# Three rewrites of a hybrid GDN / differential-attention layer and a later place for the projection's stores

## The chip, the cores and the metric

The kernel runs on one core of a Trainium2 chip, as one program with one launch. The metric is the device time of a run in microseconds (us), the median of several runs. A core has five instruction queues that run beside each other, each in its own order: PE (TensorE, matrix products and transposes), ACT (ScalarE), DVE (VectorE), POOL (GpSimd) and SP, which here issues every DMA transfer. Matrix results land in PSUM, in eight banks of 128 x 512 float32; everything else stands in SBUF or in DRAM.

## The reference

One decoder layer with 2048 tokens, model width 1024 and two groups of four heads that read the same normalised input, all in float32:

```python
hn = rms_norm(x, w_norm)
proj = einsum("bsd,de->bse", hn, w_in)          # q_a k_a v_a z_a b_a a_a q_b k_b v_b z_b
# A: gated DeltaNet, 4 heads, chunks of 64
qkv = silu(causal_depthwise_conv(q_a|k_a|v_a, conv_w)); q_a, k_a = l2_norm(..), l2_norm(..)
a_mat = tril(k_beta k^T * decay, -1) + I
u, w = solve_triangular(a_mat, [v_beta, k_beta * exp(g)])
state = state * exp(g_last) + k_dec^T (u - w state);  o_a = q_dec state + tril(q k^T * decay) v_new
o_a = rms_norm(o_a, gdn_norm_w) * silu(z_a)
# B: differential attention, 4 heads, two 64-wide maps each, causal
q_b, k_b = rope(rms_norm(q_b)), rope(rms_norm(k_b))
p = softmax(q1 k1^T / 8) - lam * softmax(q2 k2^T / 8);  o_b = p v_b
o_b = rms_norm(o_b, subln_w) * (1 - lam_init) * silu(z_b)
out = x + concat(o_a, o_b) w_out
```

## The kernel before

**How products are made.** A float32 operand is used in one of two ways. As plain float32 a product is issued as one matrix instruction that the chip runs as two passes (the profile shows both). Or it is split into a high part that TensorE reads in its reduced float32 form (`fp32r`) and the rest, and the product is the sum of three single passes: high x high, high x rest, rest x high. The projection, the scores, the output product and the chunk products of part A are three-product sums; the attention's second product (probabilities x values, "AV"), the triangular inverse and the state scan are plain float32.

**Stages.** (1) `x_scale` and `x_split` normalise and transpose the input; `in_proj` runs three passes over column groups of `w_in` and halves of the tokens. One job is one PSUM bank `psi` (three of them) of 24 or 48 matrix instructions. Three generators `epilogue` take the jobs in turn; each has one buffer `raw` and one `acc`, evicts the bank on ACT, works on it, and stores it to DRAM (`za_s`, `gdx`, `qk`, `v`, `zb_s`). An epilogue begins its next job only when its store has landed. (2) Part A runs beside the projection: `gdn_a` makes chunk products, `gdn_fs` inverts the 32 x 32 diagonal blocks on DVE, `gdn_comp` loads them back in another layout, `gdn_inv` joins 32 to 64 and 64 to 128 for each of 32 units (16 chunks x 2 head pairs), `gdn_scan` carries the state, `gdn_out` norms, gates and stores. (3) When both are done, attention runs over 32 units of 256 queries (four heads x blocks b = 0..3, then four heads x b = 4..7): `att_scores`, `att_exp`, `att_combine` (p1 and p2 are scaled and summed), `att_tr` (transposes and evicts p as `th`), `att_mm` (AV), `att_norm`. The output product `out_mm` fills PE's gaps and makes the end.

**What sets the order.** All stages are Python generators, and `Flow` (lines 34 to 223) is a planner that runs them: every `yield engine, wait, condition` is a piece for one engine; the planner holds a modelled clock for each engine and takes the piece that could start first (rounded to 100 ns, then by priority). The instructions are recorded in that order, and each engine runs its own queue strictly in that order, SP too. So a modelled wait shifts where an instruction stands, and nothing else.

**Names.** `psi`, `psb`, `pss`, `psg`, `tp` are PSUM tiles; `hh`/`hl` the split input, `wh`/`wl` the split weights, `wr` the raw ones; `vv` a value tile; `Ti`, `Tn`, `z` (z1, z2), `comp`, `lr` belong to the inverse. All matrix instructions go through one helper (L140, transposes L152), all ACT, DVE and POOL instructions through another (L81), all transfers through L161, so the profile's groups are told apart by tile names.

Of the kernel before, what the change touches and what calls it, by code (L numbers as in the profile page):

```python
# [12 lines left out]
ALU = mybir.AluOpType  # L13
# [213 lines left out]
def hybrid_kernel(ctx: ExitStack, tc: tile.TileContext, x, w_norm, w_in, conv_w, a_log, dt_bias,  # L227
# [23 lines left out]
    v_s = [dram.tile([S, 2 * P], F32, name=f"v_{j}") for j in range(2)]  # L251
# [12 lines left out]
    NOW = -5000  # L264

# [109 lines left out]
    NW, NX5, NXB, NTI, NLR = 264, 3, 2, 4, 4  # L375
# [254 lines left out]
    def epilogue(par, of):  # L630
        t_f = 0.0
        for n in range(par, NJ, of):
# [9 lines left out]
            if kind == GA:  # L642
# [12 lines left out]
                yield "SP", None, None  # L655
# [3 lines left out]
            elif kind == GD_:  # L659
# [19 lines left out]
                yield "SP", None, None  # L679
# [3 lines left out]
            elif kind == GQ:  # L683
# [44 lines left out]
                yield "SP", None, None  # L728
# [4 lines left out]
            elif kind == GV:  # L733
                vv = raw([P, 2, 256])
                act.activation(vv, ps.rearrange("p (t c) -> p t c", t=2), AF.Copy)
                fl.release("I")
                yield "SP", None, None
                ts_ = slice((t0 + what[0]) * P, (t0 + what[0] + 2) * P)
                t_f = dma(out=v_s[arg][ts_, :].rearrange("(t p) d -> p t d", p=P), in_=vv)
                n_v[arg] += 1  # L740
            else:
                ac = acc([P, TB])
                act.activation(ac, ps, AF.Silu)
                fl.release("I")
                yield "POOL", None, None
                pool.tensor_tensor(out=ac, in0=ac, in1=sub.to_broadcast([P, TB]), op=ALU.mult)
                yield "SP", None, None
                t_f = dma(out=zb_s[arg * 2 + what][:, ts_], in_=ac)
                n_zb[arg * 2 + what] += 1
# [193 lines left out]
    def gdn_fs():  # L943

        for sg_ in range(2):
# [20 lines left out]
            dma(out=d_s[sg_][:, 0], in_=T.rearrange("p j i -> p (j i)"))  # L966
            t_fs[sg_] = dma(out=d_s[sg_][:, 1], in_=X.rearrange("p j i -> p (j i)"))
            n_fs[0] += 1

    n_comp, t_comp = [0], [0.0]  # L970

    def gdn_comp():
        for ib in range(4):
            yield "SP", (lambda: t_fs[ib // 2]), lambda: n_fs[0] > ib // 2 and n_T[0] >= 8 * ib
            for h in range(H):
                if h % 2 == 0:
                    comp[h // 2] = ga.tile([P, 2, 4, 2, 32], F32, name=f"comp{h // 2}")
                for a in range(4):
                    r0 = h * 32 + a * 8 + ib % 2 * 4
                    t_comp[0] = dma(out=comp[h // 2][a * 32:(a + 1) * 32, h % 2].rearrange("p c t i -> p (c t) i"),  # L980
                                    in_=d_s[ib // 2][r0:r0 + 4].rearrange("c t (j i) -> j (c t) i", i=32), run=32)
                yield "SP", NOW, None
            n_comp[0] += 1
# [52 lines left out]
    def gdn_inv():  # L1036

        yield "POOL", NOW, lambda: n_fs[0] > 0  # L1040
        z1 = ga.tile([P, 2, 2, 32], F32, name="z1")
        z2 = ga.tile([P, 2, 64], F32, name="z2")
        nc.gpsimd.memset(z1, 0.0)
        nc.gpsimd.memset(z2, 0.0)
        last = None
        for u in units_b + [None]:
            t_d = t_z = t_n = 0.0
            if u is not None:
                c, hp = u
                yield "POOL", (lambda: t_comp[0]), lambda: n_comp[0] > c // 4 and len(Tt) < NTI  # L1050
                dl, du = (comp[hp][:, :, c % 4, i] for i in range(2))
# [5 lines left out]
                Tn = ga.tile([64, 2, 64], F32, name="Tn", bufs=2)  # L1057
                pool.tensor_tensor(out=Tn.rearrange("p h (a i) -> p h a i", i=32),
                                   in0=dl[:64, :, None, :].to_broadcast([64, 2, 2, 32]),
                                   in1=blk[:64, None, 0:2, None].to_broadcast([64, 2, 2, 32]), op=ALU.mult)  # L1060
                t_n = fl.after("ACT")
                yield "PE", (lambda: max(LR[hp, c][1], last[3] if last else 0.0)), lambda: (hp, c) in LR, "+G"
                lr = LR[hp, c][0]
            else:
                yield "PE", (lambda: last[3]), None, "+G"
            p1_ = ps_g.tile([P, 2, 96], F32, name="psg")
            if u is not None:
                for hh in range(2):
                    mm(out=p1_[:64, hh, 64:], lhsT=lr[:, hh, 64:], rhs=dl[:, hh], start=True, stop=True)
            if last is not None:  # L1070
                _, llr, lTn, _ = last
                for hh in range(2):
                    mm(out=p1_[:64, hh, :64], lhsT=llr[:64, hh, :64], rhs=lTn[:, hh], start=True, stop=True)
                live_l[0] -= 1
                t_l[0] = max(t_l[0], fl.after("SP"))
            t_1 = fl.after("DVE")
            yield AC
            if u is not None:
                act.activation(z1[32:64, :, 0], p1_[0:32, :, 64:], AF.Copy)
            if last is not None:  # L1080
                act.activation(z2[64:128], p1_[:64, :, :64], AF.Copy)
            t_z = fl.after("PE")
            if u is not None:
                yield "DVE", (lambda: t_1), None
                dve.tensor_copy(out=z1[96:128, :, 1], in_=p1_[32:64, :, 64:])
            fl.release("G")
            t_z = max(t_z, fl.after("PE"))
            yield "PE", (lambda: t_z), None, "+G"
            p2_ = ps_g.tile([P, 2, P], F32, name="psg")
            if u is not None:  # L1090
                for hh in range(2):
                    mm(out=p2_[:32, hh, 64:96], lhsT=du[:, hh], rhs=z1[:, hh, 0], start=True, stop=True)
                for hh in range(2):
                    mm(out=p2_[:64, hh, 96:], lhsT=z1[:, hh].rearrange("p b i -> p (b i)"), rhs=du[:, hh],
                       start=True, stop=True)
            if last is not None:
                lT = Tt[last[0]]
                for hh in range(2):
                    mm(out=p2_[:64, hh, :64], lhsT=z2[:, hh], rhs=lT[:, hh, 64:128], start=True, stop=True)
            t_2 = fl.after("DVE")  # L1100
            yield "ACT", (lambda: max(t_2, t_n)), None
            if last is not None:
                act.activation(lT[0:64, :, 64:128], p2_[:64, :, :64], AF.Copy)
                t_T[last[0]] = fl.after("PE")
            if u is not None:
                act.activation(Tn[32:64, :, 0:32], p2_[0:32, :, 64:96], AF.Copy)
                t_n = fl.after("PE")
                yield "DVE", (lambda: max(t_2, t_d)), None
                dve.tensor_copy(out=T[0:32, :, 32:64], in_=p2_[0:32, :, 96:])
                dve.tensor_copy(out=T[64:96, :, 96:128], in_=p2_[32:64, :, 96:])  # L1110
                last = (hp, c), lr, Tn, max(t_n, fl.after("PE"))
# [85 lines left out]
    def gdn_out():  # L1197
        for c in range(NC):
# [7 lines left out]
            rq = ga.tile([P, H], F32, name="rq")  # L1206
            rs = ga.tile([P, H], F32, name="rs")
            mh = mhalf.to_broadcast([P, H])
            pool.tensor_scalar(out=rq, in0=ssq, scalar1=EPS, scalar2=None, op0=ALU.add)
            pool.tensor_tensor(out=rq, in0=rq, in1=mh, op=ALU.pow)  # L1210
            yield PO
            pool.tensor_scalar(out=rq, in0=rq, scalar1=P ** -0.5, scalar2=None, op0=ALU.mult)
            pool.tensor_tensor(out=rs, in0=rq, in1=rq, op=ALU.mult)
            pool.tensor_tensor(out=rs, in0=rs, in1=sso, op=ALU.mult)
# [522 lines left out]
```

## Time and profile before

| | |
|---|---|
| time, median of 3 runs | 1535.0 us (1533.8 to 1536.4) |
| the profiled execution's own time | 1530.73 us |
| its span, first to last instruction | 1529.0 us |
| mean granted TensorE clock | 0.989 |
| busy: PE / DVE / ACT / POOL | 1480.3 / 958.1 / 812.4 / 497.0 us |
| DMA | 240.44 MB, 157 GB/s |

Busy time is a union: two overlapping instructions count once. Matrix instructions overlap in the pipeline, so the duration that a row gives for one (some 0.3 to 0.4 us) is longer than what it takes from the engine; the distance from one start to the next is what it costs when they run back to back. In the timeline a row is one group of equal instructions: start, length, engine, line, what is written and read, shape, count, and in brackets the idle time before it with what ended it.

### The profile page before, as it was taken

The page shows a single profiled execution, that of the slowest core. Times are in us where ns is not written, and L with a number is a line of the kernel's source. Part 1 is how long each engine was busy: PE and PEld are TensorE (multiplying, and loading weights), DVE is VectorE, ACT ScalarE, POOL GpSimd, SP SyncE. Part 2 cuts the span into 40 slices and gives each one's busy share as a digit, 9 for nine tenths or more (in the row PEclk, how much of TensorE's full clock was granted, in tenths as well). Part 3 has the DMA queues.
Part 4 walks back from the last instruction along what each step waited for, and adds up shares of the span by engine and source line. Part 5 has one row for each costly group of instructions (what it writes and reads, how often), then busy time and mean ns, then how long its engine had stood idle before and what let it go on. Part 6 is the DMA issues. An engine that isn't in the chain of part 4 may idle for free.

```text
span 1529.0 us, 27274 instructions
## 1 busy us (share of the span) xinstructions
PE 1480.3 (97%) x9671; PEld 1269.1 (83%) x9671; DVE 958.1 (63%) x2577; ACT 812.4 (53%) x1797; POOL 497.0 (33%) x616
## 2 busy tenths in 40 slices
PE   8799998999999999999999999999999999999899
PEld 6788888888789899998899899877777777877677
DVE  6466875569766667682444552227778778587782
ACT  5354464453565445323446642138777677676762
POOL 3311234500435646545353576411111122110011
PEclk8899999999999999999999999999999999999999
DMA  8758556874854774768876357256565263624224
GB/s 204 155 165 196 166 167 115 173 173 95 176 145 121 172 187 151 178 131 229 262 156 174 117 143 176 73 189 204 187 200 163 93 200 104 214 79 139 80 92 147
DMA packets 265864, 240.44 MB, mean 157 GB/s; under 512 B 46672, under 2 KB 235776, under 8 KB 263680
## 3 DMA queue, kind: packets, MB, share of 16 engines
q1 hardware_dynamic: 265728, 238.71, 57.7%
q8 instruction: 76, 1.25, 0.3%
q14 instruction: 60, 0.49, 0.1%
HBM read 150.57 MB, written 88.08 MB: 156 GB/s over the span
## 4 chain that ended last, share of the span: by engine, by line
PE 71%; DMA 10%; DVE 8%; POOL 4%; ACT 3%; issue 2%; SPq 2%; DVEq 0%; POOLq 0%; ACTq 0%
PE psi L140 32%; PE psb L140 18%; PE psg L140 7%; PE pss L140 7%; PE psb L152 4%; DMA wr<-in_w_in_dram 3%; SPq L161 2%; PE psg L152 2%; DVE p L81 2%; DMA x<-gdx 1%; DVE acc L81 1%; DMA wr<-in_w_out_dram 1%; POOL rqx L81 1%; PE tp L152 1%; POOL t L81 1%
## 5 line engine op out<-in xcount | busy, mean ns | idle before, releaser
L140 PE MATMUL psi<-wh,hh 128*128 128x256 f32 (+1 forms) x1024 | 307.7, 301 | 11.3 <-ACT acc L81 8.2
L140 PE MATMUL psi<-wl,hh 128*128 128x256 f32 (+1 forms) x1024 | 292.6, 286 | 4.7 <-DVE wl L81 4.6
L140 PE MATMUL psi<-wh,hl 128*128 128x256 f32 (+1 forms) x1024 | 291.8, 285 | 0.0
L81 DVE TENSOR_SCALAR_CACHE_REDUCE p<-pss 128x512 f32<-128x512 f32 (+3 forms) x320 | 179.3, 605 | 75.9 <-DMA kk<-qk 42.0
L140 PEld LDWEIGHTS psi<-wh,hh 128*128 128x128 f32 x1024 | 198.1, 193 | 13.0 <-ACT acc L81 8.6
L140 PE MATMUL psi<-hh,wh 128*128 128x512 f32 x512 | 206.0, 402 | 0.0
L140 PEld LDWEIGHTS psi<-wl,hh 128*128 128x128 f32 x1024 | 198.2, 194 | 5.8 <-DVE wl L81 5.1
L140 PE MATMUL psi<-hh,wl 128*128 128x512 f32 x512 | 202.4, 395 | 0.0
L140 PE MATMUL psi<-hl,wh 128*128 128x512 f32 x512 | 201.7, 394 | 0.0
L140 PEld LDWEIGHTS psi<-wh,hl 128*128 128x128 f32 x1024 | 197.5, 193 | 0.0
L81 ACT ACTIVATE p<-p,nm 128x128 f32<-128x128 f32 (+15 forms) x128 | 153.0, 1199 | 46.6 <-DVE nm L81 35.2
L81 ACT ACTIVATE raw<-psi 128x512 f32<-128x512 f32 x96 | 57.1, 595 | 141.0 <-PE psi L140 134.6
L140 PE MATMUL psb<-th,vv 128*128 128x256 f32 (+1 forms) x576 | 131.2, 369 | 0.0
L140 PE MATMUL pss<-kk,QQ 64*128 64x512 f32 (+3 forms) x960 | 123.3, 382 | 4.7 <-DVE p L81 2.7
L81 DVE SCALAR_TENSOR_TENSOR acc<-raw,cw,acc 128x512 f32<-128x512 f32 x144 | 113.3, 787 | 16.2 <-ACT acc L81 14.0
L140 PEld LDWEIGHTS psb<-th,vv 128*128 128x128 f32 x576 | 104.5, 190 | 13.0 <-issue 1.1
L140 PEld LDWEIGHTS psi<-hh,wl 128*128 128x128 f32 x512 | 96.2, 188 | 22.4
L140 PEld LDWEIGHTS pss<-kk,QQ 64*128 64x128 f32 x960 | 80.3, 184 | 41.2 <-DVE p L81 13.0
L140 PEld LDWEIGHTS psi<-hh,wh 128*128 128x128 f32 x512 | 96.2, 188 | 20.6
L140 PEld LDWEIGHTS psi<-hl,wh 128*128 128x128 f32 x512 | 96.4, 188 | 20.2
L140 PE MATMUL psb<-woh,oh 128*128 128x512 f32 x256 | 110.3, 431 | 0.0
L81 POOL TENSOR_TENSOR zb<-zb,sq 128x256 f32<-128x256 f32 x32 | 24.1, 754 | 261.1 <-DVE sq L81 215.9
(211 smaller groups left out, 3053.2 us busy)
## 6 DMA issues: line engine op xcount, KB each, us to landing
wr<-in_w_in_dram SPq DMA_DIRECT2D x80, 256.0 KB
x<-gdx SPq DMA_DIRECT2D x32, 512.0 KB
wr<-in_w_in_dram SPq DMA_DIRECT2D x24, 512.0 KB
gdx<-acc SPq DMA_DIRECT2D x48, 256.0 KB
kk<-qk SPq DMA_DIRECT2D x48, 256.0 KB
qk_a<-gdx SPq DMA_DIRECT2D x32, 256.0 KB
qk<-raw SPq DMA_DIRECT2D x32, 256.0 KB
qk<-acc SPq DMA_DIRECT2D x32, 256.0 KB
```

Of the source, the lines that this page charges most:

```text
L81: return call(*args, **kw)
L140: return self.nc.tensor.matmul(out=out, lhsT=lhsT, rhs=rhs, **kw)
L152: return self.nc.tensor.transpose(out=out, in_=in_, identity=identity)
L161: self.nc.sync.dma_start(out=out, in_=in_, **kw)
```

## The change

It has four parts.

- **Spread inverse joins** (`gdn_inv`, `gdn_comp`, `gdn_fs`). Before, a unit takes two PE pieces, each followed by evictions. Now there is one PE piece and one PSUM tile per step, and a step holds four units at different stages: the first product of the next unit, the two middle products of this one, and two products of the two before it. All products have 64 stationary columns and 128 contraction rows (`Tn` is now a 128-row tile whose lower half is zero, the 32-column product takes both blocks of `comp`). The loads of `comp` are split by head pair, `Ti` has five buffers for four.
- **Three-product AV**. The projection's epilogue stores values as two tensors (high and rest, one DVE subtraction more for each of 16 jobs); `v_load` loads two tiles; `att_tr` evicts `th` always on ACT and then the rest `tl` on DVE; `att_mm` issues three `fp32r` passes where one float32 product stood. In `att_combine` DVE takes no part any more: ACT or POOL scales p1 (by a balance of modelled loads), ACT scales p2, POOL adds, over pieces of up to 2048 columns for 1024.
- **One-power norm** (`gdn_out`). The two nested inverse roots are folded into one: four POOL instructions in place of eight for each of 16 chunks.
- **Stores** (`ST`). The epilogues' stores are planned 2.5 us after their data is ready, so loads that are due in that time stand ahead of them in SP's queue.

```diff
+    ST = ("SP", 2500, None)
@@ epilogue (the same at each of its five stores)
-                yield "SP", None, None
+                yield ST
@@ epilogue, values
-                vv = raw([P, 2, 256])
-                act.activation(vv, ps.rearrange("p (t c) -> p t c", t=2), AF.Copy)
+                vh, vl = raw([P, 2, 256]), acc([P, 2, 256])
+                psv = ps.rearrange("p (t c) -> p t c", t=2)
+                act.activation(r(vh), psv, AF.Copy)
+                yield DV
+                dve.tensor_tensor(out=r(vl), in0=psv, in1=vh, op=ALU.subtract)
                 fl.release("I")
...
-                t_f = dma(out=v_s[arg][ts_, :].rearrange("(t p) d -> p t d", p=P), in_=vv)
+                for i, vv in enumerate((vh, vl)):
+                    t_f = dma(out=v_s[i][arg][ts_, :].rearrange("(t p) d -> p t d", p=P), in_=vv)
@@ gdn_inv: one step (ua: next unit, ub: this one, ud, ue: the two before)
+            ps = ps_g.tile([P, 2, 224], F32, name="psg")
...
+                    mm(out=ps[:64, hh, 0:32], lhsT=LR[ha, ca][0][:, hh, 64:], rhs=comp[ha][:, hh, ca % 4, 1],
+                       start=True, stop=True)
...
+                    mm(out=ps[:64, hh, 32:64], lhsT=comp[hp][:, hh, c % 4].rearrange("p t i -> p (t i)"),
+                       rhs=z1[:, hh, 0], start=True, stop=True)
+                for hh in range(2):
+                    mm(out=ps[:64, hh, 64:96], lhsT=z1[:, hh].rearrange("p b i -> p (b i)"), rhs=du[:, hh],
+                       start=True, stop=True)
...
+                    mm(out=ps[:64, hh, 96:160], lhsT=LR[hd, cd][0][:, hh, :64], rhs=Tns[(k - 1) % 2][:, hh],
+                       start=True, stop=True)
...
+                    mm(out=ps[:64, hh, 160:], lhsT=z2[:, hh], rhs=Te[:, hh, 64:128], start=True, stop=True)
@@ gdn_out
-            pool.tensor_scalar(out=rq, in0=ssq, scalar1=EPS, scalar2=None, op0=ALU.add)
-            pool.tensor_tensor(out=rq, in0=rq, in1=mh, op=ALU.pow)
...
+            pool.tensor_scalar(out=rs, in0=ssq, scalar1=EPS * P * P, scalar2=EPS * EPS * P * P, op0=ALU.mult,
+                               op1=ALU.add)
+            pool.tensor_tensor(out=rs, in0=rs, in1=sso, op=ALU.add)
...
+            pool.tensor_tensor(out=rs, in0=rs, in1=mhalf.to_broadcast([P, H]), op=ALU.pow)
@@ att_combine
-    WAYS = ("ADd",)
+    WAYS = ("AAP", "PAP",)
-    CB = 1024
+    CB = 2048
@@ att_tr
-            e = fl.pick(ACT=478, DVE=602)
-            yield e, None, None
+            yield AC
             for a, q_ in regs:
...
+                act.activation(th[:, a, q_], pt[:, a, q_], AF.Copy)
+            yield DV
+            for a, q_ in regs:
+                dve.tensor_tensor(out=tl[:, a, q_], in0=pt[:, a, q_], in1=f(th[:, a, q_]), op=ALU.subtract)
@@ att_mm
-                    mm(out=po[:, q_], lhsT=V[:, k % 4], rhs=th[:, j, q_], start=(k == 0), stop=last)
+                    mm(out=po[:, q_], lhsT=vh_, rhs=th[:, j, q_], start=(k == 0), stop=False)
+                    mm(out=po[:, q_], lhsT=vh_, rhs=tl[:, j, q_], start=False, stop=False)
+                    mm(out=po[:, q_], lhsT=vl_, rhs=th[:, j, q_], start=False, stop=last)
```

The letters of a way name the engine that scales p1, the one that scales p2 and the one that adds (a small `d`: DVE scales p2 and adds in one instruction).

The change alters the places of instructions on every engine. Three of them matter below. First PE, in the joins of the inverse; before, one unit is two pieces, with projection products (`psi`) between them. The first piece:

```order
L140 MATMUL psi<-wh,hl 128x256
L140 MATMUL psg<-comp_8892,lr 64x32 x2
L140 MATMUL psg<-Tn,lr 64x64 x2
L140 MATMUL psi<-wh,hh 128x256
L140 MATMUL psi<-wl,hh 128x256
```

and the second piece, some fifteen rows later:

```order
L140 MATMUL psi<-wh,hl 128x256
L140 MATMUL psg<-z_3872,comp_8892 32x32 x2
L140 MATMUL psg<-comp_8892,z_3872 64x32 x2
L140 MATMUL psg<-Ti,z_3873 64x64 x2
L140 MATMUL psg<-S_9899,x_9828 128x128
```

After the change PE has one piece of ten products a step:

```order
L140 MATMUL psg<-rr_8312,Ti 128x128
L140 MATMUL psg<-comp_7854,lr 64x32 x2
L140 MATMUL psg<-z_3845,comp_7757 64x32 x2
L140 MATMUL psg<-comp_7757,z_3845 64x32 x2
L140 MATMUL psg<-Tn_3848,lr 64x64 x2
L140 MATMUL psg<-Ti,z_3846 64x64 x2
L140 MATMUL psg<-vh_8338,kv_8270 128x128
```

The count of products is the same; they stand together, and the 32 x 32 product has become one of 64 rows.

Second PE, in attention: transposes of p (`ident,p`) and AV. Before, with one product per 128 keys (`vv` holds the values):

```order
L152 MATMUL psb<-ident,p_15360 128x128
L152 MATMUL psb<-ident,p_15528 128x128 x2
L140 MATMUL psb<-th_15679,vv 128x256 x2
L140 MATMUL psb<-th_15686,vv 128x256 x2
L140 MATMUL psb<-th_15717,vv 128x256 x2
L140 MATMUL psb<-th_15723,vv 128x256
L140 MATMUL psb<-th_15723,vv 128x128
```

After it, with three (`v_13586` is the high part of the values, `v_13588` the rest):

```order
L152 MATMUL psb<-ident,p_14472 128x128
L152 MATMUL psb<-ident,p_14614 128x128
L152 MATMUL psb<-ident,p_14472 128x128
L152 MATMUL psb<-ident,p_14614 128x128
L140 MATMUL psb<-th_15021,v_13586 128x256
L140 MATMUL psb<-tl_15022,v_13586 128x256
L140 MATMUL psb<-th_15021,v_13588 128x256
L140 MATMUL psb<-th_15021,v_13586 128x256
L140 MATMUL psb<-tl_15022,v_13586 128x256
L140 MATMUL psb<-th_15021,v_13588 128x256
```

A product of before is one row and two passes; each row of after is one pass, so 576 passes become 864.

Third ACT, some 30 us into the program, where the first jobs' banks are evicted into `acc` (the numbers tell buffers in order of time). Before:

```order
L81 ACTIVATE acc_459<-psi 128x256
L81 ACTIVATE hh<-tp 128x4x128 x2
L81 ACTIVATE acc_510<-psi 128x256
L81 ACTIVATE hh<-tp 128x4x128 x2
L81 ACTIVATE tp,ssqx_551<-xt 128x512 x2
L81 ACTIVATE wh<-wr 128x1056
L81 ACTIVATE hh<-tp 128x4x128
L81 ACTIVATE acc_602<-psi 128x256
```

After:

```order
L81 ACTIVATE acc_461<-psi 128x256
L81 ACTIVATE hh<-tp 128x4x128 x2
L81 ACTIVATE tp,ssqx_518<-xt 128x512 x2
L81 ACTIVATE hh<-tp 128x4x128 x2
L81 ACTIVATE wh<-wr 128x1056
L81 ACTIVATE hh<-tp 128x4x128 x2
L81 ACTIVATE acc_594<-psi 128x256
L81 ACTIVATE acc_604<-psi 128x256
L81 ACTIVATE acc_635<-psi 128x256
```

The fourth eviction (`acc_510` before, `acc_594` after) now stands behind the cast of the second weights. It needs the first epilogue's store, which SP issued between the second weights' two halves and now issues after all constants, 14 rows later in its queue.

## Rows read from the trace of the kernel before

**Rows 1.** Busy time by engine in stretches; columns are named in the first row.
```profile
core 0: us, PE busy (x) PEld busy (x) DVE busy (x) ACT busy (x) POOL busy (x), PEclk, DMA share, GB/s
0.00:65.00 65.00, 49.97 (x327) 44.32 (x327) 39.21 (x61) 33.60 (x81) 23.38 (x37) 0.87 0.82 189
...
400.00:900.00 500.00, 488.80 (x3879) 450.67 (x3878) 287.58 (x784) 242.34 (x777) 258.66 (x362) 0.99 0.64 165
...
1155.00:1498.00 343.00, 337.21 (x2026) 263.81 (x2025) 258.90 (x735) 241.94 (x373) 47.33 (x43) 1.00 0.40 128
```

**Rows 2.** Groups by form on PE: shape, count, busy us, mean ns, idle before.
```profile
L140 PE MATMUL psb<-th,vv 128*128 128x256 f32 x512 | 124.1, 381 | 0.0
L152 PE MATMUL psb<-ident,p 128*128 128x128 f32 x544 | 75.1, 274 | 2.7 <-DVE xr L81 1.7 <-DVE p L81 0.6
...
L140 PE MATMUL psb<-th,vv 128*128 128x128 f32 x64 | 12.3, 274 | 0.0
```

**Rows 3.** Timeline of PE in attention: start, length, instructions.
```profile
1252.83 2.75 PE L140 MATMUL psb<-th,vv 128*128 128x256 f32 x12
1255.42 1.47 PE L152 MATMUL psb<-ident,p 128*128 128x128 f32 x12
1256.73 0.82 PE L140 MATMUL psb<-th,vv 128*128 128x256 f32 x4
```

**Rows 4.** Timeline of PE beside the inverse, from 476.8 us.
```profile
476.81 0.42 PE L140 MATMUL psg<-comp,lr 128*64 128x32 f32 x4
...
477.53 0.49 PE L140 MATMUL psg<-vh,kv 128*128 128x128 f32 x2
...
478.21 0.28 PE L140 MATMUL psi<-wh,hh 128*128 128x256 f32 x1
...
479.16 0.28 PE L140 MATMUL psi<-wh,hl 128*128 128x256 f32 x1
479.37 0.31 PE L140 MATMUL psg<-z,comp 128*32 128x32 f32 x4
479.61 0.42 PE L140 MATMUL psg<-comp,z 128*64 128x32 f32 x4
479.87 0.42 PE L140 MATMUL psg<-Ti,z 128*64 128x64 f32 x4
480.22 0.66 PE L152 MATMUL psg<-ident,og 128*128 128x128 f32 x4
```

**Rows 5.** Groups by form on ACT, attention.
```profile
L81 ACT ACTIVATE th<-psb 128x512 f32<-128x512 f32 x95 | 52.9, 595 | 26.2 <-PE psb L152 25.7
L81 ACT ACTIVATE p<-p,sc 128x1024 f32<-128x1024 f32 x40 | 45.7, 1149 | 15.0 <-DVE sc L81 14.8
```

**Rows 6.** Groups by form on DVE, attention.
```profile
L81 DVE SCALAR_TENSOR_TENSOR p<-p,sc,p 128x1024 f32<-128x1024 f32 x40 | 54.4, 1367 | 12.9 <-ACT p L81 12.8
L81 DVE TENSOR_TENSOR xr<-psb,xr 128x512 f32<-128x512 f32 x64 | 43.9, 685 | 24.0 <-PE psb L140 22.0 <-DMA out_dram<-xr 1.3 <-DMA xr<-in_x_dram 0.5
```

**Rows 7.** Groups by form on POOL, whole program.
```profile
L81 POOL TENSOR_TENSOR acc<-acc,sub 128x512 f32<-128x512 f32 x16 | 17.9, 1122 | 52.7 <-ACT acc L81 49.7 <-issue 3.0
...
L81 POOL TENSOR_TENSOR wl<-wr,wh 128x1024 fp32r<-128x1024 f32 x4 | 9.8, 2441 | 21.0 <-ACT wh L81 21.0
```

**Rows 8.** Timeline of PE, first 65 us: instructions after an idle time.
```profile
47.72 0.39 PE L140 MATMUL psi<-wh,hh 128*128 128x256 f32 x1 [3.02 <-ACT acc L81]
63.30 0.59 PE L140 MATMUL psi<-wh,hh 128*128 128x264 f32 x1 [5.17 <-ACT acc L81]
```

**Rows 9.** Timeline of ACT in the same stretch.
```profile
47.28 0.38 ACT L81 ACTIVATE acc<-psi 128x256 f32<-128x256 f32 x1 [5.36 <-DMA za_s<-acc]
...
61.91 1.06 ACT L81 ACTIVATE wh<-wr 128x1024 fp32r<-128x1024 f32 x1 [8.54 <-DMA wr<-in_w_in_dram]
```

**Rows 10.** Who waited for whom: us in total, times, longest us.
```profile
POOL zb L81 <- DVE sq L81: 215.9, 27, 23.4
ACT raw L81 <- PE psi L140: 134.6, 64, 5.1
```

More of the change, by code (lines that the diff above doesn't have):

```diff
@@ L250, in hybrid_kernel @@
     qk_s = [[dram.tile([P, 2, S], F32, name=f"qk{i}_{h}") for h in range(H)] for i in range(2)]
[L251 removed]
+    v_s = [[dram.tile([S, 2 * P], F32, name=f"v{i}_{j}") for j in range(2)] for i in range(2)]
     za_s = dram.tile([S, 512], F32, name="za_s")
@@ L1042, in gdn_inv @@
         z2 = ga.tile([P, 2, 64], F32, name="z2")
[L1043 to L1051, printed above, removed]
+        Tns = [ga.tile([P, 2, 64], F32, name=f"Tn{i}") for i in range(2)]
+        for t in (z1, z2, *Tns):
+            nc.gpsimd.memset(t, 0.0)
+        unit = lambda k: units_b[k] if 0 <= k < len(units_b) else None
+        t_z1 = t_z2 = t_n = t_d = 0.0
+        for k in range(-1, len(units_b) + 2):
+            ua, ub, ud, ue = (unit(k + 1 - i) for i in range(4))
+            if ub is not None:
+                c, hp = ub
+                yield "POOL", (lambda: t_comp[hp]), lambda: len(Tt) < NTI
+                du, dl = (comp[hp][:, :, c % 4, i] for i in range(2))
                 T = Tt[hp, c] = ga.tile([P, 2, P], F32, name="Ti", bufs=NTI)
@@ L1062, in gdn_inv @@
[L1062 to L1067, printed above, removed]
+                t_p = fl.after("ACT")
+            yield ("PE", (lambda: max(t_z1, t_z2, t_n, *((LR[ua[1], ua[0]][1], t_comp[ua[1]]) if ua else ()))),
+                   lambda: ua is None or (ua[1], ua[0]) in LR and n_comp[ua[1]] > ua[0] // 4, "+G")
@@ L1068, in gdn_inv @@
+            ps = ps_g.tile([P, 2, 224], F32, name="psg")
+            if ua is not None:
+                ca, ha = ua
                 for hh in range(2):
-                    mm(out=p1_[:64, hh, 64:], lhsT=lr[:, hh, 64:], rhs=dl[:, hh], start=True, stop=True)
-            if last is not None:
-                _, llr, lTn, _ = last
+                    mm(out=ps[:64, hh, 0:32], lhsT=LR[ha, ca][0][:, hh, 64:], rhs=comp[ha][:, hh, ca % 4, 1],
+                       start=True, stop=True)
+            t_1 = fl.after("DVE")
@@ L1074, in gdn_inv @@
+            if ud is not None:
+                cd, hd = ud
+                for hh in range(2):
+                    mm(out=ps[:64, hh, 96:160], lhsT=LR[hd, cd][0][:, hh, :64], rhs=Tns[(k - 1) % 2][:, hh],
+                       start=True, stop=True)
+                LR.pop((hd, cd))
                 live_l[0] -= 1
                 t_l[0] = max(t_l[0], fl.after("SP"))
[L1076 to L1090, printed above, removed]
-                for hh in range(2):
[L1092 to L1106, printed above, removed]
-                t_n = fl.after("PE")
[L1108 to L1111, printed above, removed]
+            if ue is not None:
+                Te = Tt[ue[1], ue[0]]
+                for hh in range(2):
+                    mm(out=ps[:64, hh, 160:], lhsT=z2[:, hh], rhs=Te[:, hh, 64:128], start=True, stop=True)
@@ new lines, in gdn_inv @@
+            t_2, t_2d = fl.after("ACT"), fl.after("DVE")
+            yield "ACT", (lambda: max(t_2, t_p) if ub else t_2), None
+            if ub is not None:
+                act.activation(Tn[32:64, :, 0:32], ps[0:32, :, 32:64], AF.Copy)
+                t_n = fl.after("PE")
+            if ud is not None:
+                act.activation(z2[64:128], ps[:64, :, 96:160], AF.Copy)
+                t_z2 = fl.after("PE")
+            if ua is not None:
+                act.activation(z1[32:64, :, 0], ps[0:32, :, 0:32], AF.Copy)
+                t_z1 = fl.after("PE")
```

89 lines of the change are left out of this document (47 added, 42 removed).

## The prediction

> **What bounds the kernel now.** I read the busy time by stretch first. PE is at work for 488.80 of 500 us while part A runs beside the projection, and for 337.21 of 343 us in attention's wide half (blocks b = 4..7); only the first 65 us show a real hole, 49.97 of 65 [rows 1]. No other engine comes near: in the wide half DVE has 258.90, ACT 241.94 and POOL 47.33 of 343 us. So time is what PE's stream of passes takes, plus a few stalls, and an edit on another engine counts only if it makes PE wait. The second view is the groups on PE by form, for how many passes the change touches [rows 2]; the third is the timeline, because the durations of passes (0.27 to 0.38 us) overlap and only the distance between starts is a price [rows 3, 4]. Last come the stalls at the start and the waits [rows 8 to 10].
>
> **AV.** 288 float32 products are 576 passes: 512 of 256 columns and 64 of 128 [rows 2]. Twelve of the first kind start at 1252.83 and the next instruction at 1255.42, so one costs 0.216 us; twelve transposes of 128 columns take 1256.73 - 1255.42 = 1.31, so 0.109 each, and I give the 128-column passes that price [rows 3]. Before: 512 x 0.216 + 64 x 0.109 = 117.6 us. After there are three `fp32r` passes for each product. Their price stands in the projection, which streams 256 columns with new weights at every pass: from 478.21 to 479.16 there are eight, 0.119 each [rows 4]. After: 768 x 0.119 + 96 x 0.109 = 101.9 us. The term is **-16 us**. Between -12 and -24: half of the float32 price, 0.108, is the least that 256 columns can be given from these rows; four us for mixing with other shapes is my allowance the other way.
>
> The rows say that three passes cost 0.357 where float32 costs 0.432. [...]
>
> **Joins of the inverse.** Before, a unit's first piece runs from 476.81 to 477.53, the second from 479.37 to 480.22, and entering one costs 0.21 - 0.12 = 0.09 more than a pass (479.16 to 479.37) [rows 4]: 0.72 + 0.85 + 2 x 0.09 = 1.75 us. After, a step has ten products or twenty passes of 64 columns. Four of these took 479.61 to 479.87, 0.065 each; leaving costs 480.22 - 479.87 - 0.26 = 0.09 [rows 4]. So 1.30 + 0.09 + 0.09 = 1.48, and 32 units give **-9 us**. At 0.060 a pass (479.37 to 479.61, its change of shape within) it is -12; if each cost 0.0875, as the last four with their exit did, it is +6. The evictions behind a step (four on ACT, three on DVE) were there before. A unit now takes four steps to leave; five `Ti` buffers let the joins run ahead of the scan, and PE has projection passes to put between.
>
> **The start.** Twice PE waits for the release of a `psi` bank, 3.02 us at 47.72 and 5.17 at 63.30 [rows 8]. The first ends when ACT, which waits 5.36 us for the landing of a `za_s` store, evicts; the second when ACT comes free of the second `wh` cast, for whose weights it waits 8.54 us [rows 9]. In the new order the first epilogue's store has moved behind the constants, so the fourth eviction, which had been done by then, joins that first wait. PE runs dry one job sooner, 24 x 0.119 = 2.9 us. The second `wh` cast has moved from ACT to DVE, but ACT then waits in its place for the last two tiles of x, queued behind about as many bytes. I take **+3 us**; -8 if both stalls go, +6 if two jobs are missing.
>
> **Attention's other engines.** In the wide half (51200 columns of p, 104 of 144 steps) I charge whole rows, without their fixed part. ACT scales p2 too except where POOL scales p1 (26240 columns): 24960 more at 1149/1024 = 1.122 ns, 28 us; and all evictions `th`, 27 of 176 from DVE, 0.595 each, 12 us [rows 5]. DVE loses the scale-and-add, 51200 x 1367/1024 ns = 68 us, and gets 104 subtractions at 0.685 (the same shape and sources as `xr`), 71 us [rows 6]. POOL gets the adds at 2441/1024 = 2.38 ns, 122 us, and 26240 x 1122/512 = 58 us [rows 7]. The stage shrinks by 104/144 of AV's 16 us to 331; ACT 282 (85%), DVE 262 (79%), POOL 227 (69%) [rows 1]. PE still bounds. But the way of one tile gets longer: for 2048 columns from 1.15 + 2 x 1.37 = 3.9 us (ACT and DVE in halves) to 4.6 + 4.9 = 9.5 (two scalings, then POOL) or 4.5 + 4.9 = 9.4 (POOL twice). A tile has 343/32 = 10.7 us of PE time and there are three buffers of the second map, so 5.5 us more lies within them. PE's transposes of p, which wait for this way, idle 2.7 us now [rows 2]; for a way twice as long I add as much again, **+3 us**. Bare, 32 x 5.5 = 176; at best 0.
>
> **At no cost.** The values' extra subtraction (16 x 0.685 = 11 us of DVE) holds a bank longer; ACT waits 134.6 us in all for banks to be filled, so banks come free early enough [rows 10]; uncovered it is those 11 us. Ten and a half MB more of transfers (16 stores, 24 loads of 256 KB) fall where the DMA share is 0.40 to 0.64 [rows 1]. The norm's four saved instructions are POOL's, which works 258.66 of 500 us there, and PE does not wait behind it. The stores after the start could give at most the 11.2 us that PE idles from 400 to 900, or cost, say, three stalls of the 3.02 kind, 9 us; I take 0, the middle of the two.
>
> **Sum.** -16 - 9 + 3 + 3 = -19 us on the profiled execution's 1530.7 (span 1529.0): 1511.7. That execution lies 4.3 below the median of 1535.0, so **1516**. A difference of 0.2%, 3 us, is about what a measurement tells from no change.
>
> **Rivals.** [...]
> (C) *POOL takes PE's place in the wide half, and the kernel gets slower*. POOL's queue is strict: a norm's multiply on `zb` that waits for DVE (215.9 us in 27 waits, the longest 23.4 [rows 10]) has nothing behind it today; now it has scalings and adds. If on the 17 wide tiles that POOL both scales and adds half of the extra 5.5 us shows, it is 47 us: 1516 - 3 + 47 = **1560**. It decides from 22 us, or 0.7 us for each of 32 wide tiles. Against: POOL is 69% loaded and PE has output products to put in between. [...]
> (D) *The stores eat it*: an epilogue that waits longer for its landing keeps ACT, hence a bank, hence PE. Six stalls of 3.02 us give all back: **1534**, no change. The same time results if the new passes cost 0.144 and save nothing while the joins gain little, which the evenly spaced projection speaks against.
>
> **How the numbers follow.** Forecast 0.64 (its own range 1507 to 1525), B 0.20, C 0.08, D 0.08. Eight in ten lie between 1500 and 1532: the forecast and B reach 1500 by AV at -24 or joins at -12, and the upper end takes half of D. Faster 0.84 (forecast, B), same 0.08 (D), slower 0.08 (C).
>
> **What would show it.** Starts of AV passes 0.12 us apart, 864 of them; joins in groups of twenty passes of some 1.4 us; one PE stall near 45 us that is longer than 3 us; PE busy over 98% of the wide half with POOL near 225 us. Transposes that idle behind POOL's `p` for more than 20 us would make the forecast wrong, and so would stalls of PE behind ACT evictions after 65 us that the trace of before does not have.

## The result and the profile after

The changed kernel takes 1508.3 us (median of 4 runs, 1504.7 to 1509.3) against 1535.1; the ratio is 0.982 (0.980 to 0.984). Forecast were 1516 (1500 to 1532) and "faster". Its profiled execution takes 1508.30 us, span 1506.6: 22.4 below that of before, where the sum said 19.

The stretches that answer to [rows 1], busy time by engine:

```profile
core 0: us, PE busy (x) PEld busy (x) DVE busy (x) ACT busy (x) POOL busy (x), PEclk, DMA share, GB/s
0.00:65.00 65.00, 48.88 (x313) 43.76 (x314) 41.60 (x65) 33.34 (x80) 23.75 (x40) 0.85 0.78 190
400.00:900.00 500.00, 479.39 (x3892) 448.80 (x3891) 290.19 (x786) 242.44 (x777) 236.46 (x301) 0.99 0.63 173
1145.00:1475.00 330.00, 328.52 (x2312) 267.57 (x2311) 254.86 (x813) 279.61 (x403) 217.49 (x99) 1.00 0.48 149
```

The wide half of attention is the last row. The stretch of before was 343 us long and this one is 330 (331 forecast), and PE idles 1.5 us in it for 5.8. The two stretches don't hold quite the same work (218 value products before, 228 here); attention as a whole, from its first score to the end, takes 497.3 us for 515.3. In the stretch of 330 us ACT, DVE and POOL work 280, 255 and 217 us; 282, 262 and 227 were forecast. The middle row went the other way: PE idles 20.6 of 500 us in the projection's stage, for 11.2 [rows 1].

The groups that answer to [rows 2]:

```profile
L140 PE MATMUL psb<-th,v 128*128 128x256 f32 x512 | 114.0, 296 | 0.2 <-DVE tl L81 0.2
L152 PE MATMUL psb<-ident,p 128*128 128x128 f32 x544 | 78.3, 274 | 2.1 <-DVE tl L81 1.4 <-DVE sq L81 0.4 <-DVE lrec L81 0.2
L140 PE MATMUL psb<-tl,v 128*128 128x256 f32 x256 | 71.4, 279 | 0.0
...
L140 PE MATMUL psb<-th,v 128*128 128x128 f32 x64 | 14.3, 248 | 0.0
...
L140 PE MATMUL psb<-tl,v 128*128 128x128 f32 x32 | 8.8, 275 | 0.0
```

There are 864 passes, and the transposes idle 2.1 us, not the 5 to 6 that the longer way was to cost. PE's timeline shows the price of a pass (start, length):

```profile
1311.81 0.36 PE L140 MATMUL psb<-th,v 128*128 128x256 f32 x1
1312.01 0.28 PE L140 MATMUL psb<-tl,v 128*128 128x256 f32 x1
1312.12 0.40 PE L140 MATMUL psb<-th,v 128*128 128x256 f32 x2
...
1313.18 0.28 PE L140 MATMUL psb<-th,v 128*128 128x256 f32 x1
1313.30 0.49 PE L152 MATMUL psb<-ident,p 128*128 128x128 f32 x3
```

From 1312.01 to 1313.30 there are eleven, 0.117 each (0.119 taken from [rows 4], 0.216 for a float32 pass in [rows 3]). One step of the joins, twenty passes from 504.23 to 505.51, 1.28 us (1.30 forecast), answers to [rows 4]:

```profile
504.23 0.39 PE L140 MATMUL psg<-comp,lr 128*64 128x32 f32 x4 [0.77 <-DVE Ti L81]
504.45 0.40 PE L140 MATMUL psg<-z,comp 128*64 128x32 f32 x4
504.69 0.40 PE L140 MATMUL psg<-comp,z 128*64 128x32 f32 x4
504.92 0.42 PE L140 MATMUL psg<-Tn,lr 128*64 128x64 f32 x4
505.18 0.40 PE L140 MATMUL psg<-Ti,z 128*64 128x64 f32 x4
505.51 0.71 PE L140 MATMUL psg<-rr,Ti 128*128 128x128 f32 x4
```

**The account.** Both streams are close to the forecast, and yet the parts don't add up one by one (below). To see why, I split each span in three: PE's idle time (span less PE busy), what the clock cost (span times one less the mean granted clock), and the rest, PE's work at full clock. For the changed kernel the mean granted clock is 0.984: 1506.6 - 1453.5 = 53.1 idle, 0.016 x 1506.6 = 24.1 lost, 1429.4 work. The clock's third digit makes each split uncertain by 0.8 us, and two things make it coarser. The split charges half-clock time even where PE idled in it; the last column charges it only where PE was busy. And each row is a single execution: the changed kernel, "tl first" and the two kernels with stalls and transposes put into attention (below) have the same instructions in the same order ahead of attention, and yet they lose 60 to 73 us there to idle time and clock. "Ratio" is to before on the same chip, with its 95% interval.

| kernel | median us | ratio | idle | clock | work | work, clock charged where PE was busy |
|---|---|---|---|---|---|---|
| before | 1535.1 | 1 | 48.7 | 16.8 | 1463.5 | 1466.1 |
| changed | 1508.3 | 0.982 (0.980-0.984) | 53.1 | 24.1 | 1429.4 | 1432.1 |
| joins alone | 1538.9 | 1.003 (1.002-1.005) | 60.9 | 29.2 | 1445.5 | 1449.9 |
| AV alone | 1524.3 | 0.993 (0.992-0.995) | 56.0 | 22.8 | 1444.3 | 1448.2 |
| stores alone | 1557.5 | 1.015 (1.013-1.017) | 63.7 | 35.8 | 1458.9 | 1465.3 |
| changed, stores as before | 1509.9 | 0.985 (0.983-0.986) | 56.5 | 18.1 | 1433.4 | 1435.4 |
| changed, joins as before | 1511.7 | 0.984 (0.982-0.987) | 48.2 | 16.6 | 1443.2 | 1447.0 |
| changed, stores at 1.5 us | 1508.1 | 0.982 (0.980-0.985) | 57.2 | 21.1 | 1427.9 | 1431.9 |
| changed, tl first | 1506.2 | 0.981 (0.978-0.985) | 55.3 | 16.5 | 1432.1 | 1433.5 |

The work adds up within some 7 us: joins take 18 from before and 14 from the kernel without them, AV 19 from before and 12 from joins alone (to the changed kernel with stores as before). By the last column joins take 16 and 15, AV 18 and 14. Idle time and clock, 65.5 us together before, run from 65 to 100. An order that doesn't change scatters by some 13 of these, so only the larger steps, above all the 34 of the stores alone, can be put down to a part.

**Where the clock is lost.** Six of PE's stalls in the changed kernel, with the idle time before each in brackets; the first two answer to [rows 8]:

```profile
39.35 0.90 PE L152 MATMUL tp<-ident,x 128*128 128x128 f32 x3 [3.64 <-ACT tp L81]
60.92 0.59 PE L140 MATMUL psi<-wh,hh 128*128 128x264 f32 x1 [5.11 <-ACT acc L81]
...
486.30 0.61 PE L140 MATMUL psg<-comp,lr 128*64 128x32 f32 x4 [2.26 <-DMA lr<-l_s]
...
659.52 0.85 PE L152 MATMUL tp<-ident,t 128*128 128x128 f32 x4 [4.55 <-POOL t L81]
...
884.35 0.55 PE L152 MATMUL psg<-ident,x 128*128 128x128 f32 x3 [2.00 <-DMA x<-gdx]
...
946.69 0.69 PE L152 MATMUL tp<-ident,t 128*128 128x128 f32 x2 [2.28 <-POOL t L81]
```

Just ahead of the fourth, and just behind it (columns as in the first fence):

```profile
650.00:655.00 5.00, 4.96 (x42) 4.76 (x41) 4.86 (x12) 0.60 (x1) 0.03 (x1) 1.00 0.71 135
659.80:663.20 3.40, 3.40 (x19) 3.40 (x18) 2.84 (x8) 0.60 (x1) 2.65 (x3) 0.51 0.27 90
```

PE is busy all through the second row, but at a granted clock of 0.51, and issues 19 passes in 3.4 us where 42 went through in 5. Passes of one kind show it best, in the stretch and just behind it:

```profile
660.38 0.41 PE L140 MATMUL psi<-wl,hh 128*128 128x256 f32 x1
660.59 0.41 PE L140 MATMUL psi<-wh,hl 128*128 128x256 f32 x1
...
663.32 0.28 PE L140 MATMUL psi<-wh,hh 128*128 128x256 f32 x1
663.45 0.28 PE L140 MATMUL psi<-wl,hh 128*128 128x256 f32 x1
663.56 0.28 PE L140 MATMUL psi<-wh,hl 128*128 128x256 f32 x1
```

A pass takes 0.21 us in it and 0.12 behind it. So the stall costs its 4.55 us and nearly half of such a stretch besides.

### The profile page after: what moved, and what is told of

Same layout as the page of the kernel before. It is cut to its first block, busy times and chain, and to the rows that moved or that the text cites. A ratio compares the mean times of both kernels' runs of the same rounds, so it can differ in the third digit from the quotient of the medians.

```text
span 1506.6 us, 28239 instructions
## 1 busy us (share of the span) xinstructions
PE 1453.5 (96%) x9959; PEld 1266.6 (84%) x9959; DVE 954.8 (63%) x2641; ACT 848.2 (56%) x1819; POOL 700.3 (46%) x662
## 4 chain that ended last, share of the span: by engine, by line
PE 53%; DMA 4%; DVE 3%; ACT 2%; POOL 2%; issue 1%; SPq 0%; ACTq 0%; POOLq 0%; DVEq 0%
PE psb L140 18%; PE psi L140 16%; PE pss L140 8%; PE psg L140 5%; PE psb L152 4%; PE psg L152 1%; DMA qk<-acc 1%; DMA x<-gdx 1%; PE tp L152 1%; DMA v<-raw 1%; POOL rqx L81 1%; ACT p L81 1%; DMA wr<-in_w_in_dram 1%; DVE p L81 1%; POOL t L81 1%
## 5 line engine op out<-in xcount | busy, mean ns | idle before, releaser
L81 POOL TENSOR_TENSOR p<-p,p 128x640 f32<-128x640 f32 (+9 forms) x64 | 162.4, 2541 | 63.2 <-ACT p L81 61.1
L81 ACT ACTIVATE raw<-psi 128x512 f32<-128x512 f32 (+1 forms) x96 | 56.9, 595 | 126.3 <-PE psi L140 101.0
L140 PE MATMUL psb<-th,v 128*128 128x256 f32 (+1 forms) x576 | 123.1, 291 | 0.2 <-DVE tl L81 0.2
L81 DVE TENSOR_TENSOR tl<-psb,th 128x512 fp32r<-128x512 f32 (+2 forms) x176 | 92.6, 563 | 40.7 <-ACT th L81 39.2
L81 ACT ACTIVATE p<-p,sc 128x384 f32<-128x384 f32 (+15 forms) x89 | 109.6, 1248 | 13.6 <-DVE sc L81 9.0
L140 PEld LDWEIGHTS psi<-hh,wl 128*128 128x128 f32 x512 | 96.0, 188 | 22.4
L140 PEld LDWEIGHTS pss<-kk,QQ 64*128 64x128 f32 x960 | 81.6, 187 | 35.8 <-issue 8.1
```

Source lines behind the costliest of these rows:

```text
L81: return call(*args, **kw)
L140: return self.nc.tensor.matmul(out=out, lhsT=lhsT, rhs=rhs, **kw)
```

## The experiments

**The parts alone.** Each is the kernel before with one part of the diff, or the changed kernel with one part taken back; the stores' lines are

```diff
-    ST = ("SP", 2500, None)
+    ST = ("SP", None, None)
```

where stores stand as before. Joins alone:

> The kernel before with the spread joins alone. Theory 1: PE's matrix time of the joins falls from 57 us (51.0 in the groups and 66 entries of 0.09) to about 47; the projection's stage gives some of it back in waits, since after the whole change it ends only 3.6 us earlier: 1526 to 1532 us. Rival (the spread joins shorten the wait of the scan too): the stage from 400 to 1010 us shrinks by more than the joins' 10 us, under 1524 us. Third: nothing (1533 to 1537), because a unit takes longer to leave and the scan waits for it as long as PE saves.

Measured: 1538.9 us. No theory had it that slow. PE's work fell by 18 us, and idle time and clock rose by 12.2 and 12.4, more than it gave. AV alone:

> The kernel before with the three-product AV and its combine on ACT and POOL alone (joins, norm and stores as before). Theory 1 (PE's stream of passes is the time): the attention stage from its first score to the end shrinks by about 16 to 19 us and the projection stage does not change, so 1516 to 1519 us, some two thirds of the whole change. Rival (the joins and the load order make the change; AV's saved passes are lost to the longer way of a tile): not more than 8 us faster, over 1527 us, with PE idle in the wide half above the 5.8 us of before.

Measured: 1524.3, between the theories. The work fell by 19 us, more than forecast; 13 came back as idle time and clock, ahead of attention: from its first score to the end that takes 494.8 us against 515.3 before, but it begins 14.5 us later. Stores alone:

> The kernel before with the projection's stores planned 2.5 us later and nothing else. Theory 1: loads were not waited for much, so within 3 us of before (1532 to 1538), with the stall near 40 us no shorter than 3 us. Rival (loads that stand ahead of the stores come in time and close PE's stalls from 200 to 900 us): 4 to 10 us faster, 1525 to 1531.

Measured: 1557.5, slower than every theory. PE's stalls in its trace, three of the long ones:

```profile
635.84 0.58 PE L140 MATMUL psi<-wl,hh 128*128 128x256 f32 x1 [5.71 <-DVE wl L81]
...
854.28 0.83 PE L152 MATMUL psg<-ident,x 128*128 128x128 f32 x3 [3.28 <-DMA x<-gdx]
...
1427.49 1.73 PE L140 MATMUL pss<-kk,QQ 64*128 64x512 f32 x6 [2.52 <-DMA kk<-qk]
```

None names a store: the first waits for a split of weights, the others for loads of x and of the keys. Idle time (15 us more) and clock (19 us more) make the loss, while the work hardly moved (by 1 us in the last column). Of the 29 us of this execution 18 came ahead of attention and 11 in it, where no store of the projection stands. That the new places in the queue shift what PE needs is my reading; how a store's place leads to these stalls was not traced. Everything but the stores:

> The changed kernel with the stores planned as before (joins, AV and norm kept). Theory 1: within 3 us of the changed kernel's 1508 (1505 to 1511). Rival (the stores' place is worth several us): 1512 to 1518. If the place of the stores in fact costs something, 1500 to 1504.

Measured: 1509.9, as theory 1 had it. The stores' part costs 23 us alone and nothing that shows within the whole. It has no price of its own.

**Joins taken back, stores at another time.**

> The changed kernel without the spread joins (the inverse, its loads and its four Ti buffers as before); three-product values, norm and stores as changed. Theory 1 (the joins' shorter stream is PE time wherever it stands): slower than the changed kernel by 7 to 12 us, 1515 to 1520. Rival (the parts change the order of the projection's stage, and the stalls and half-clock stretches of an order outweigh the stream; alone the joins cost 5 us, the stores 23): no sum of parts holds, and the time can lie anywhere from 1505 to 1540; then PE's idle time plus what the granted clock cost, read from its trace, account for the difference, not the joins' 10 us.

Measured: 1511.7, 3.4 slower by the medians (the intervals overlap), less than either number of theory 1. The joins are worth 13.8 us of work here, and 12.4 went into stalls and clock: in its trace PE is busy for 489.01 of the 500 us from 400, as it was before, and for 479.39 with the joins (473 to 479 in the four executions with that order). This is the rival's account, though its range of 35 us excluded little and single executions scatter by as much as the 12.4.

> The changed kernel with the epilogues' stores planned 1.5 us after their data in place of 2.5. No instruction is added or removed; only the order of the queues shifts. Theory 1 (the order of the stores is worth little, as forecast): within 3 us of the changed kernel, 1505 to 1511. Rival (the order of the projection's stage is worth more than an edit of it: every order has other stalls of PE, each followed by a stretch at the lower clock): the time moves by 4 us or more either way, with the difference in idle time of PE and in the granted clock before attention, and attention's own length unchanged within 3 us.

Measured: 1508.1. Theory 1 holds: a microsecond less changes nothing once all parts are in, so not every shift of the order is a new draw.

**The combine as before.**

```diff
-    WAYS = ("AAP", "PAP",)
+    WAYS = ("ADd",)
-    CB = 2048
+    CB = 1024
```

> The changed kernel with the scaling and adding of p as it was before: DVE scales p2 and adds in one instruction, over pieces of 1024 columns; everything else as changed. Theory 1 (the forecast's account of the wide half): the relief of DVE is what lets the three-product passes pay. DVE had 254.86 us of work in 330 there; with the scale-and-add back it has some 68 us more, 323 of 330, and it bounds: attention gets longer by 10 us or more, 1518 to 1545. Rival (PE's stream alone decides, the shorter way through ACT and DVE is as good as the longer one through POOL): within 4 us of the changed kernel, 1504 to 1512.

Measured: 1531.9, 24 us slower than the changed kernel (ratio to before 0.997, 0.994 to 0.999). The time is theory 1's and rules the rival out; that it is DVE that bounds was not read from a trace. Here the three passes pay only together with the new combine.

**The rest first.**

```diff
-  mm(out=po[:, q_], lhsT=vh_, rhs=th[:, j, q_], start=(k == 0), stop=False)
-  mm(out=po[:, q_], lhsT=vh_, rhs=tl[:, j, q_], start=False, stop=False)
+  mm(out=po[:, q_], lhsT=vh_, rhs=tl[:, j, q_], start=(k == 0), stop=False)
+  mm(out=po[:, q_], lhsT=vh_, rhs=th[:, j, q_], start=False, stop=False)
```

> The changed kernel with the first two of the three passes of a value product exchanged: the rest of p (tl) first, its high part second. 85 of 288 passes on tl start more than 0.17 us after the pass before them, which is 0.1 us later than the others: 5 to 9 us in all. Theory 1 (a pass that has to wait for a semaphore of its own costs 0.1 us even where the data is there; with tl first one wait covers both): 1500 to 1504. Rival (the late start is that of the first pass of a pair, whose record begins before the transposes ahead of it have ended, so nothing is lost): same as the changed kernel, 1506 to 1510.

Measured: 1506.2 (1503.2 to 1509.3), not to be told from the changed kernel, and its attention takes 497.0 us for 497.3. The rival holds: in this trace, too, 85 passes start late, and they are again the second of the three, now on `th`. So the late start at 1312.01 above goes with the place behind a first pass, not with `tl`, and nothing is lost by it.

**A stall by itself, and the same place filled.** In each of attention's 16 wide units, before the first AV pass (without the `for` in the first kernel):

```diff
+  nc.tensor.matmul(out=po[:96, :96], lhsT=dd, rhs=dd, start=True, stop=True)
+  nc.sync.dma_start(out=dd, in_=c_ident[:, :96])
+  for _ in range(30):
+      nc.tensor.transpose(out=po[:, :P], in_=ident, identity=ident)
+  nc.tensor.matmul(out=po[:96, :96], lhsT=dd, rhs=dd, start=True, stop=True)
```

> The changed kernel with a stall of PE put into each of the 16 wide units of attention: one product reads a small tile dd, a 48 KB load then overwrites dd, and a second product that reads dd makes PE wait for the load to land. Nothing else is changed, the order of all queues stays. Theory 1 (a stall costs its own length): the length of one stall, read from this trace, times 16, and no more; at 2 to 2.5 us each with the two products some 35 to 45 us, 1543 to 1553. Theory 2 (each stall is followed by a stretch at the lower granted clock, as after the stalls of 2 us and more in the traces so far, 3.4 us or longer): the stalls and another 1.7 us or more each, 27 us or more in all, 1570 or above; the granted clock of the wide half falls from 1.00 to about 0.9.

Measured: 1579.4 (ratio 1.028, 1.024 to 1.032), 71 us over the changed kernel. One of the stalls, on PE's timeline:

```profile
1466.94 0.64 PE L1534 MATMUL psb<-dd 128*96 128x96 f32 x2 [5.32 <-DMA dd<-in_ident_dram]
1467.28 0.56 PE L140 MATMUL psb<-th,v 128*128 128x256 f32 x1
1467.64 0.41 PE L140 MATMUL psb<-tl,v 128*128 128x256 f32 x1
...
1468.28 0.41 PE L140 MATMUL psb<-tl,v 128*128 128x256 f32 x1
...
1470.78 0.28 PE L140 MATMUL psb<-tl,v 128*128 128x256 f32 x1
```

and the wide half of this kernel, then of the filled one:

```profile
1150.00:1545.00 395.00, 347.95 (x2316) 286.22 (x2315) 245.81 (x775) 274.97 (x393) 212.86 (x96) 0.94 0.38 120
```

```profile
1150.00:1548.00 398.00, 389.66 (x2860) 327.11 (x2859) 255.73 (x816) 281.52 (x404) 217.96 (x99) 1.00 0.41 127
```

From 1467.64 to 1468.28 three passes take 0.213 each; by 1470.78 the distance is back to 0.117. The 16 stalls sum to 45.8 us (1.7 to 5.3 each), longer than either theory took them; the 32 products cost some 7 (0.222 each, measured below). That leaves some 18 us that length alone doesn't explain, and the wide half's clock is 0.94: over the changed kernel's attention, the half clock takes 19 us more while PE is at work. The time is in theory 2's range, but its 27 us for the clock were too many, since only 12 of the 16 stalls had such a stretch.

> The same 16 places with the same two products and load, but between the two PE runs 30 transposes of the identity, which need nothing. PE is then away from the kernel's work for longer than in the stalls, 30 x 0.109 = 3.3 us each. Theory 2 (what costs is that PE stood still, by the clock afterwards): no stretch at the lower clock, 16 x (3.3 + 0.4) = 59 us over the changed kernel at most, 1555 to 1570, and so no slower than the true stalls, though each is longer. Theory 1 (only the length counts): slower than the stalls by 16 x about 1 us, 15 us or more.

Measured: 1581.3, above theory 2's range by 11 us, but only 1.9 over the stalls (theory 1: 15 or more). The granted clock stays at 1.00. The work is 59 us over the changed kernel's, as worked out; idle time rose by 13.6, 6.3 of it before attention begins, where nothing was changed, and 7.1 at seven of the places, where the load took longer than the transposes. Only the longest of these seven waits was followed by a stretch at the lower clock (3.4 us):

```profile
1472.01 0.41 PE L1534 MATMUL psb<-dd 128*96 128x96 f32 x2 [2.46 <-DMA dd<-in_ident_dram]
```

Attention alone takes 562.4 us with the places filled, 568.1 with the stalls and 497.3 without either: PE is away from its work for longer and loses less. (Attention with nothing put into it took 492.9 to 497.3 in four executions.)

**Filling the kernel's own stalls.** A product with zeros is added to the open sum, so many times, after so many projection products:

```diff
+    n_psi, FILL = [0], {0: 13, 114: 17, 216: 24, 973: 13}
...
+        for _ in range(FILL.pop(n_psi[0], 0)):
+            nc.tensor.matmul(out=o, lhsT=ident, rhs=zz, start=new, stop=new)
```

> The changed kernel with passes that add nothing (a product with a tile of zeros) at four of its stalls, where PE would only wait: before the first projection product (13 of them, 2.77 us of waiting), after 114 (17, 3.64 us), after 216 (24, 5.11 us) and after 973 (13, 2.84 us). The order of all other work stays. Theory 2 (a stall is followed by a stretch at half clock: 6.8, 6.8, 6.8 and 3.4 us of it stand behind these four): up to half of these stretches comes back, 12 us, less where the next stall takes the time up again because a load sets it: 1498 to 1505. Theory 1 (the stalls cost their length alone): nothing is gained, 1506 to 1512.

Measured: 1504.9 (ratio 0.979, 0.976 to 0.982; the changed kernel's is 0.982). Its first 65 us, busy time by engine:

```profile
0.00:65.00 65.00, 55.66 (x418) 50.24 (x419) 39.75 (x64) 33.28 (x80) 22.10 (x39) 0.97 0.76 188
```

The clock there rose from 0.85 to 0.97, but the product behind the last wait of the first 285 us, this kernel's first and the changed kernel's second,

```profile
284.65 0.39 PE L140 MATMUL psi<-wh,hh 128*128 128x264 f32 x1 [1.42 <-DVE ab L81]
```

```profile
284.37 0.39 PE L140 MATMUL psi<-wh,hh 128*128 128x264 f32 x1 [1.42 <-DVE ab L81]
```

stands where it stood. At the start PE waits for what other engines and loads deliver, and half clock costs nothing there. What the medians differ by can't be told from scatter: in the profiled executions it lies in attention (492.9 us for 497.3), where nothing was changed. The same in the stage where PE binds:

```diff
+    n_psi, FILL = [0], {1986: 13, 2994: 26, 3900: 12, 4338: 13}
```

> The changed kernel with passes that add nothing (products with a tile of zeros) at four stalls in the middle of the projection's stage, where PE is at work 96% of the time and nothing but PE's own queue seems to hold it back: 13 ahead of the stall at 486 us (2.26 us, the wait for lr), 26 at 659 (4.55, POOL's t), 12 at 884 (2.00, the load of x), 13 at 946 (2.28, POOL's t). The order of all other work stays. Theory 2 (a stall brings a stretch at half clock, and where PE bounds that stretch is lost time): the stretches of 6.8, 3.4, 3.4 and 3.4 us behind them give back half, up to 8.5 us, less what the passes overrun: 1500 to 1505. Theory 1 (the clock is not what costs, or a later wait takes the gain up as it did at the start of the program): no gain, 1506 to 1513.

Measured: 1502.8 (1502.0 to 1507.2; ratio 0.981, 0.978 to 0.983). The stall at 659 in this trace, filled:

```profile
655.70 0.28 PE L140 MATMUL psi<-wh,hl 128*128 128x256 f32 x1
655.82 5.94 PE L583 MATMUL psi<-zz,ident 128*128 128x96 f32 x52
661.60 0.60 PE L152 MATMUL tp<-ident,t 128*128 128x128 f32 x4
661.95 0.36 PE L140 MATMUL psi<-wh,hh 128*128 128x256 f32 x1
662.15 0.28 PE L140 MATMUL psi<-wl,hh 128*128 128x256 f32 x1
```

The clock behind all four is full (behind this one the passes stand 0.12 us apart; over the 500 us from 400 the mean is 1.00). From 1985 projection products to the last, PE takes 518.3 us for 521.2, though the 128 passes took 14.2 (0.111 each; at this place 1.2 more than the stall). But four other executions with the same order and nothing filled in this stretch take 517.6, 519.0, 522.5 and 527.0 us, so the 2.9 us may be scatter. And a wait for DVE at 647, 1.08 us in the changed kernel, is 2.62 here, with a half-clock stretch of its own behind it: PE leaves it no earlier after the 1985 products than it did, so what the first filling gained is gone there. By medians it is the fastest kernel, 5.5 us under the changed one and within theory 2's range; by the ratios, each to before as measured beside it, a gain over the changed kernel isn't shown. The trial with 16 stalls carries the price of a stall; this one doesn't.

## Why the prediction was right, and where not

- **AV, -16: right.** From start to start the AV passes and the transposes took 185.9 us and take 170.2, -15.7. A pass costs what the projection's rows said, 0.117 us for 0.119.
- **Joins, -9: right mechanism, a little small.** The products with their entries (0.09 each, from the rows) took 57.1 us and take 47.1, -10; the account gives -14 to -18, and the 4 to 8 us between are not assigned.
- **The start, +3: wrong.** The 385th projection product starts at 83.6 us for 83.2. The longer stall near 45 us isn't there. PE stalls for 3.64 us at 39.35 instead, before ACT has read a tile of x, whose landing it awaits for 4.81 us; the moved store costs ACT 1.01 us. The second stall is as forecast: ACT waits 6.13 us for other tiles of x in place of the second `wh` cast, and PE 5.11 us at 60.92 for 5.17. These rows answer to [rows 9]:

```profile
37.82 0.60 ACT L81 ACTIVATE tp<-xt 128x512 f32<-128x512 f32 x1 [4.81 <-DMA xt<-in_x_dram]
...
46.38 1.33 ACT L81 ACTIVATE acc<-psi 128x256 f32<-128x256 f32 x3 [1.01 <-DMA za_s<-acc]
...
57.33 0.60 ACT L81 ACTIVATE tp<-x 128x512 f32<-128x512 f32 x1 [6.13 <-DMA x<-in_x_dram]
```

- **The longer way through POOL and ACT, +3: wrong in sign.** The wide half idles 4 us less, and no transpose waits for POOL's `p`, so the buffers cover the way, and nothing in the trace speaks for rival C. Adds on POOL and evictions on ACT cost what I took; POOL's scaling was cheaper, 3.60 us for 2048 columns where I took 4.5, which is about the 10 us by which POOL's sum was too high. POOL's and ACT's groups, which answer to [rows 7] and [rows 5]:

```profile
L81 POOL TENSOR_TENSOR p<-p,p 128x1024 f32<-128x1024 f32 x4 | 9.6, 2398 | 1.6 <-ACT p L81 1.6
...
L81 POOL TENSOR_TENSOR p<-p,sc 128x2048 f32<-128x2048 f32 x2 | 7.2, 3602 | 3.2 <-ACT th L81 3.2
...
L81 ACT ACTIVATE th<-psb 128x512 fp32r<-128x512 f32 x112 | 62.9, 596 | 15.9 <-PE psb L152 15.1 <-DVE p L81 0.6
```

- **Stores and transfers, 0: right for the sum, wrong as a reason.** The term was bounded by the idle time there was, -11, and three stalls, +9; alone the part costs 23 us, and 19 us of clock stand against it in the account.
- **What no step had: the clock.** I priced every stall at its length. In the profiled executions work fell by 34.1 us (25 forecast), idle time rose by 4.4 and the clock's cost by 7.3, 11.7 for the two terms of 6. So the sum is near in part by luck: 9 us more gain and 6 us more loss nearly cancel. The account here charges the stretches at half; passes in one stand 0.213 us apart for 0.117 (the stalls put into attention). But it was no loss at the start, where PE waits for others: with the clock at 0.97 for 0.85 the product behind the last wait stood at 284.65 us for 284.37.
- **The offset, +4.3.** Half of the miss of 7.7 us is this: the profiled execution of before lay 4.4 under its median, the one of the changed kernel on it (1508.30 and 1508.26). The other half is the sum, -22.4 for -19.

The time lies between the forecast and B's 1504, nearer to B. B stood for the gain whole, -16 - 9 with the longer way hidden and the start unchanged, and -6 for loads that would close half of PE's 11.2 us of idle time in the projection's stage. It was right that the longer way is hidden and the start hardly changes, and wrong on the loads: there are 20.6 us of idle time now. The norm was not tried alone, and AV was not taken back from the changed kernel.

## What to carry to other kernels

Price a stall of PE as its length and, where PE is what binds, half of the time that PE then works at the lower clock: at the six stalls listed above it was 0.50 for 3.4 or 6.8 us, and the 16 stalls put into attention cost some 18 us more than their 45.8 and the products with them. Forecast a shorter stream by its passes, but check parts of a change together: where a planner deals the order anew, a part alone can cost more than it saves, and the whole still gain. Three reduced passes beat one float32 product here only together with a combine that takes its work off DVE, which makes the rest.

## What the hardware showed that I had not expected

Of the 16 stalls put into attention, 1.7 to 5.3 us long, 12 were followed by a stretch at the lower clock (in the one shown above passes 0.213 us apart for 0.117), though PE was back at work; the four that were not lasted 1.7 to 2.2 us, and others as short were. Useless passes kept the clock up, transposes (1.00 for 0.94 in the wide half) and products with zeros (0.97 for 0.85 in the first 65 us) alike. And a float32 product with a 96-column tile took 0.222 us, two passes of 0.111, as much as I had priced for 128 columns.
